# A hybrid attention and recurrence block: queries of six heads as blocks, the first head's gates beside the merge, exponentials ahead of the transposes

## The chip, the cores and the metric

One core of a Trainium2 chip runs the whole layer as one program. The metric is the device time of one execution in microseconds. TensorE (PE) multiplies, ScalarE (ACT) applies functions and copies, VectorE (DVE) does elementwise work and reductions, GpSimd (POOL) does a little of both, and SyncE (SP) issues most of the DMAs. Each engine takes its instructions strictly in the order in which they were written.

## The reference

The layer takes `x` of 1024 tokens by 1024 channels. It computes, in float32:

```
h = rms_norm(x) * norm_w
z = h @ w_in                       # 1024 x 12288: everything below is a slice of z
# branch A: three head groups, 8 heads of 64, (window, dilation) = (128,1), (512,4), (2048,16)
q, k = rms_norm(q)*q_w, rms_norm(k)*k_w
s = q k^T / 8 + bias, banded;  m = max s;  p = exp(s - m);  den = sum p;  o = p v / den
o_a = sum_g(den_g * exp(m_g - max m) * o_g) / sum_g(den_g * exp(m_g - max m))      # the merge
y_a = (o_a * silu(g_a)) @ w_proj_a
# branch B: 8 heads of 128, forward and backward scan, summed
f = lb + (1 - lb) * sigmoid(z_f)
S_t = diag(f_t) S_{t-1} + (1 - f_t) v_t^T ;  o_t = S_t^T q_t                       # in chunks
y_b = (rms_norm(o_fwd + o_bwd) * silu(g_b)) @ w_proj_b
out = x + (sigmoid(zg_a) * y_a + sigmoid(zg_b) * y_b) @ w_out
```

## The kernel before, in words

**Number format.** Every float32 operand of a large product is split into a high part (`hi`, the value rounded to the matmul's float32r) and the rest (`lo`). A product then takes three matmuls, hi by hi, hi by lo, lo by hi. A weight page is 128 by 512 (256 KB). ScalarE makes its `whi`; its `wlo` is made by VectorE, by GpSimd, or by an accumulating DMA, as `b.low` says ("dve", "pool", "dma").

**Direct projections and blocks.** `T_group` and `tok_group` project a group of 128 by 512 outputs in 8 steps of three matmuls (tile `gp`). Other columns of `w_in` go as blocks of 256 columns by all 1024 tokens, in seven quarter-size products instead of eight (`run_quads`, tiles `qA`, `qE`, `qC`), each of 4 x 3 matmuls, with sums of the input prepared once and differences of the weights made in place. The list `blocks` says which: attention's queries and keys (which are then normalised, tile `nss`), merge gates `sg`, recurrence queries `qb` of heads 0 to 3 (`QB = 4`), silu gates `gb` and `ga`. The queries of heads 4 to 7 are projected directly (`evac_qe`).

**Order of work.** One Python program writes the instructions of all engines in one pass. A planner (`Plan`) keeps an estimated time for each engine; `note` holds the costs of instructions. Work beside the main stream is a task with tiles it depends on. `tick` writes a task once its tiles are due within 1.4 us of TensorE's estimated time, and `burst` writes small products between the projection's steps, in order of their kind: transposes (kind 1), values (2), scores (3). In attention (`eager`) there is one burst after each step of three projection matmuls. So costs and due times in the planner decide the order of instructions on an engine, and the hardware then keeps to it.

**Stages.** After the input's preparation and the blocks comes attention, beside the direct projections of the recurrence's inputs (`evac_early`) and of the last heads' queries. A unit of attention is two tiles of 128 queries by four heads: `scores` (matmuls `sc` with 64 rows, bias and row maximum by VectorE), `exps` (ScalarE, four for each half), `transpose_p` (`pT`, copied out to `apt`), `pv` (matmuls `o` with 64 columns). A unit's `exps` waits for `left["turned"] == m`, which holds once all earlier units are transposed. Score tiles come from a ring of four (`s`), two for a unit; values from a ring of 14 (`VR`). Loads for later parts wait for `b.wire()`, the planner's estimate that DMAs are at most 1 us behind.

The merge (`merge_maybe`, `alphas`, `spread_al`) weighs the three groups' outputs: eight steps of three matmuls `al`, three VectorE products, a GpSimd addition, two VectorE operations and a store. Beside it run what is left of the direct projections. Then there is a barrier: `b.until(lambda: mer.get("out", 0) == 8)`, the merge's memory is given back, the recurrence's pools are opened, its lower bounds are computed (a Sigmoid and an Ln, each with its own table on ScalarE), and heads 0 to 7 follow. For each head four groups of forget gates are projected (evacuated into `sk` by `evac_f`); then `start_head` starts the recurrence of that head, which runs beside the next head's gates. The tail multiplies by `w_proj_a`, `w_proj_b`, `w_out`.

TensorE writes to eight PSUM banks, of which the projections have three (`gps`), in attention two; a group's bank is free once ScalarE has copied it out (`stage` or `sk`).

The recorded line of nearly every instruction is 58, that of the helper which passes it on and tells the planner; so the profile is read by tile names.

Of the kernel before, what the change touches and what calls it, by code (L numbers as in the profile page):

```python
# [13 lines left out]
OP = mybir.AluOpType  # L14
# [14 lines left out]
EARLY = 8  # L29
QB = 4  # L30
QRAW, SPARE = 6, 7
LOWS = ("T2", "T4")
SQ, EA = 2, 6
VR, PT = 14, 8

# [80 lines left out]
class Plan:  # L116
# [5 lines left out]
    def __init__(self, nc):  # L122
        self.nc = nc
        self.t = dict(pe=0.0, act=0.0, dve=0.0, pool=0.0, sp=0.0)
        self.port = 0.0
        self.wire = 0.0
        self.w, self.r = Book(), Book()
        self.table = "exp"
        self.wide = True
        self.pe = Engine(self, nc.tensor, "pe")  # L130
        self.act = Engine(self, nc.scalar, "act")
        self.dve = Engine(self, nc.vector, "dve")
        self.pool = Engine(self, nc.gpsimd, "pool")
        self.sp = Engine(self, nc.sync, "sp")
# [7 lines left out]
    def note(self, key, op, args, kw):  # L142
# [30 lines left out]
        else:  # L173
            if key == "pe":
                late = 0.17
                wide = ins[-1].dtype == F32R
                if op == "transpose":
                    pace = 0.109
                elif wide:
                    pace = n / 2400.0 + 0.0133 + (0.0 if self.wide else 0.15)  # L180
                else:
                    pace = 2 * (n / 1200.0 + 0.004)
                    if ins[0].shape[0] <= 64 or ins[0].shape[-1] <= 64:
                        pace /= 2
                self.wide = wide
            elif key == "act":
# [36 lines left out]
class Builder:  # L223
# [35 lines left out]

    def wire(self):  # L260

        return self.p.wire <= self.p.t["pe"] + 1.0

# [321 lines left out]
def hybrid_block(ctx, tc, a, out):  # L585
# [47 lines left out]
    for k in range(6):  # L633
        blocks += qk[2 * k:2 * k + 2] + sg[k:k + 1] + ([("qb", k)] if k % 2 == 0 and k < QB else [])
    blocks += [("gb", k) for k in range(4)] + [("ga", 0), ("ga", 2)]
# [517 lines left out]
    def attention_start(now=False):  # L1153
# [9 lines left out]
        for n, k, shape in (("v", VR, [128, 256]), ("q", 2, [128, 2, S]), ("k", 2, [128, 2, S]),  # L1163
                            ("s", 4, [128, 4, 256]), ("pt", PT, [128, 2, 2, 128]), ("os", 2, [128, 2, 2, 128]),
                            ("bias", 2, [128, 4, 256])):
            att[n] = b.ring(ap, "a" + n, k, shape)
# [4 lines left out]
        for o, g in enumerate((1, 2, 0)):  # L1171
            for hv in range(2):
                soon = lambda n, k=2 * o + hv: att[n].soon() and (k == 0 or b.wire())
                for n, f in (("k", load_k), ("q", load_q), ("bias", load_bias)):
                    b.task("sp", [], lambda g=g, hv=hv, f=f: f(g, hv), 2, lambda n=n, soon=soon: soon(n))
                for i in ((7, 0, 1, 2, 3, 4, 5, 6) if g == 0 else range(8)):
                    b.task("sp", [], lambda g=g, hv=hv, i=i: load_v(g, hv, i), 2, lambda soon=soon: soon("v"))
# [71 lines left out]
    def scores(g, hv, i0):  # L1249
# [22 lines left out]
        for u in range(2):  # L1272
# [8 lines left out]
            v_.tensor_scalar(neg[:, u], mst[g][:, 0, i0 + u, 4 * hv:4 * hv + 4], -1.0, None, op0=OP.mult)  # L1281
            b.task("act", [neg[:, u]], lambda u=u: exps(g, hv, i0, u, ss, neg, geo), 3, lambda: left["turned"] == m)
        left[g, hv] -= 1
# [93 lines left out]

    mctx = ExitStack()
    mer = {}

    def merge_maybe(now=False):
        if mer or not (now or len(stored) == 48) or not att:
            return
        if now:
            b.drain()
        b.eager, b.SLACK = False, 0.6
        psum(3)
        actx.close()
        mer["p"] = mctx.enter_context(tc.tile_pool(name="merge", bufs=1))
        mer["sel"] = sel = mer["p"].tile([128, 3, 4, 128], F32R, name="sel")  # L1390
# [82 lines left out]
    def spread_al(p, half, ld):  # L1473
# [8 lines left out]
        v_.tensor_tensor(nat(ld[1], 2), nat(al[2], 2), per(ld[2], 2), op=OP.mult)  # L1482
        g_.tensor_tensor(ld[0], ld[0], ld[1], op=OP.add)
        v_.tensor_tensor(acc, acc, ld[0], op=OP.add)
# [50 lines left out]
    for h in range(QB, EARLY):  # L1535
# [3 lines left out]
        pos += 2  # L1539
    merge_maybe(True)  # L1540
    for j in range(TAIL, LATE):
        for half in range(2):
            b.run_unit([T_group(pos, half, evac_sg(1, j, half), half == 1)])
        pos += 2
    b.until(lambda: mer.get("out", 0) == 8)
    b.drain()
    mctx.close()

    bctx = ExitStack()
    hp = bctx.enter_context(tc.tile_pool(name="hgrn", bufs=1))
    lbt = hp.tile([128, 2, 2, 8], F32, name="lbt")
    a_.dma_start(lbt, a["lb"])
    mx = hp.tile([128, 2, 8], F32, name="lbm")
    v_.tensor_tensor(mx, lbt[:, 0], lbt[:, 1], op=OP.max)
    for l in range(2):
        v_.tensor_tensor(lbt[:, l], lbt[:, l], mx, op=OP.subtract)
    v_.tensor_tensor(mx, lbt[:, 0], lbt[:, 1], op=OP.subtract)  # L1560
    lb = hp.tile([128, 2, 8], F32, name="lbv")
    omlb = hp.tile([128, 2, 8], F32, name="omlb")
    lomlb = hp.tile([128, 2, 8], F32, name="lomlb")
    a_.activation(lb, mx, AF.Sigmoid)
    v_.tensor_scalar(omlb, lb, -1.0, 1.0, op0=OP.mult, op1=OP.add)
    v_.tensor_scalar(lomlb, omlb, 1e-37, None, op0=OP.max)
    a_.activation(lomlb, lomlb, AF.Ln)
    onw = hp.tile([128, 1], F32, name="onw")
    v_.tensor_scalar(onw, hwc, 1.0 / 256, None, op0=OP.mult)
    mX = hp.tile([128, 128], F32, name="mX")  # L1570
    mY = hp.tile([128, 64], F32, name="mY")
    a_.dma_start(mX, a["c_mx"])
    a_.dma_start(mY, a["c_my"])
    BF = mybir.dt.bfloat16
    rst = hp.tile([128, 512], BF, name="rst")
    g_.memset(rst, 1.0)
    g_.memset(rst.rearrange("p (c t) -> p c t", c=4)[:, :, 0:1], 0.0)
    YB = hp.tile([128, 4, 64], F32, name="YB")
    g_.memset(YB, 0.0)

    ig_ring = b.ring(hp, "ig", 8, [128, 256])
    gb_ring = b.ring(hp, "gb", 3, [128, 512])
    sk_ring = b.ring(hp, "sk", 7, [128, 512])
    qq_ring = b.ring(hp, "q", 2, [128, 512])
# [23 lines left out]
    def load_gb(h, u):  # L1608
        t = gb_ring.get()
        s_.dma_start(t, gbD[h, u])  # L1610
        GB[h, u] = t

    SK, QQ = {}, {}

    def evac_f(h, d, u):
        def f(ps):
            t = sk_ring.get()
            a_.activation(t, ps, AF.Copy)
            b.gps.done(ps)
            SK[h, d, u] = t  # L1620
            if d == 1 and u == 1:
                start_head(h)
        return f

# [281 lines left out]
    for h in range(8):  # L1906
        if h % 2 == 0:
            load_pair(h // 2)
        for u in range(2):
            if h < EARLY:  # L1910
                b.task("sp", [qD], lambda h=h, u=u: load_q_early(h, u), 4, qq_ring.soon)
            b.task("sp", [gbD], lambda h=h, u=u: load_gb(h, u), 4, gb_ring.soon)
        for d in range(2):
            for u in range(2):
                b.run_unit([T_group(pos, u, evac_f(h, d, u), u == 1)])
            pos += 2
        if h >= EARLY:
            for u in range(2):
                b.run_unit([T_group(pos, u, evac_q(h, u), u == 1)])
            pos += 2  # L1920
# [441 lines left out]
```

## Time and profile before

| | |
|---|---|
| time, median of 3 runs | 1475.26 us (1474.36 to 1476.48) |
| the profiled execution's own time | 1474.54 us |
| its span, first to last instruction | 1472.7 us |
| granted TensorE clock, mean | 0.999 |
| busy: TensorE, VectorE, ScalarE, GpSimd | 1454.8, 964.9, 886.8, 382.4 us |
| HBM read and written | 167.98 and 81.43 MB |

Times in the profile count from the first instruction. A row of a group gives its operation, `out<-in` by tile names, shapes, count, busy time, mean duration in ns, and the idle time of the engine just before it with what ended that. Matmuls overlap in the pipeline, so that a row's mean is longer than the distance from one start to the next. A float32 matmul that is not split (`sc`, `o`, `oB`) leaves two records.

### The profile page before, as it was taken

How to read it: one execution, taken by the hardware profiler on the slowest of the kernel's cores; microseconds unless marked ns; L12 is line 12 of the kernel's file. 1: busy time of each engine (PE TensorE's matmuls, PEld its weight loads, DVE VectorE, ACT ScalarE, POOL GpSimd, SP SyncE). 2: the span in 40 equal slices, each digit the busy share in tenths (PEclk: the TensorE clock that was granted, in tenths of full speed). 3: DMA queues.
4: the chain of work that ended last, by engine and by line, in shares of the span. 5: the costliest groups of instructions: out<-in, count | busy, mean ns of one | idle time of the engine just before them, and what ended most of it. 6: DMA issues, size and time to landing. Idle time of an engine off the chain costs nothing. (4 is left out here: it accounts for less than half of the span.)

```text
span 1472.7 us, 22977 instructions
## 1 busy us (share of the span) xinstructions
PE 1454.8 (99%) x7946; PEld 1200.0 (81%) x7946; DVE 964.9 (66%) x1872; ACT 886.8 (60%) x1884; POOL 382.4 (26%) x385
## 2 busy tenths in 40 slices
PE   8999999999999999999999999999999999999998
PEld 7788888877888888887877778888888888788887
DVE  6792576778688876332535536468887976358973
ACT  5543665666576775443778743397777874548461
POOL 0031335454534333332020005332221221001011
PEclk9999999999999999999999999999999999999999
DMA  6465557667632424327657439654444453768565
GB/s 206 134 193 168 171 196 170 155 137 173 151 115 86 122 65 144 115 93 241 210 180 210 132 87 309 203 124 100 130 115 115 104 145 90 225 225 222 183 154 135
DMA packets 193896, 229.44 MB, mean 156 GB/s; under 512 B 45627, under 2 KB 117587, under 8 KB 193268
## 3 DMA queue, kind: packets, MB, share of 16 engines
q1 hardware_dynamic: 179812, 203.93, 43.8%
q0 software_dynamic: 13104, 23.86, 10.6%
q8 instruction: 63, 1.03, 0.3%
q14 instruction: 53, 0.43, 0.1%
q10 hardware_dynamic: 864, 0.19, 0.1%
HBM read 167.98 MB, written 81.43 MB: 169 GB/s over the span
## 5 line engine op out<-in xcount | busy, mean ns | idle before, releaser
L58 POOL TENSOR_TENSOR wlo<-qraw,whi 128x512 fp32r<-128x512 f32 x130 | 190.0, 1467 | 326.2 <-ACT whi L58 288.3
L58 ACT ACTIVATE whi<-qraw 128x512 fp32r<-128x512 f32 x182 | 113.0, 626 | 88.8 <-DVE qraw L58 44.8
L58 DVE TENSOR_TENSOR qraw<-qraw,qraw 128x512 f32<-128x512 f32 x104 | 93.2, 896 | 41.2 <-POOL wlo L58 31.4
L58 PE MATMUL gp<-hh,whi 128*128 128x512 f32 x288 | 118.4, 411 | 0.0
L58 PE MATMUL gp<-hh,wlo 128*128 128x512 f32 x288 | 113.1, 393 | 0.0
L58 PE MATMUL gp<-hl,whi 128*128 128x512 f32 x288 | 112.5, 391 | 0.0
L58 PE MATMUL gp<-whi,hh 128*128 128x512 f32 x248 | 103.0, 415 | 3.0 <-ACT stage L58 1.6
L58 PE MATMUL gp<-whi,hl 128*128 128x512 f32 x248 | 97.7, 394 | 1.3 <-DVE hl L58 1.3
L58 PE MATMUL gp<-wlo,hh 128*128 128x512 f32 x248 | 97.5, 393 | 0.0
L58 ACT ACTIVATE whi<-raw 128x512 fp32r<-128x512 f32 x96 | 59.9, 626 | 47.4 <-PE gp L58 26.7
L58 ACT ACTIVATE as<-as,neg 128x192 f32<-128x192 f32 (+2 forms) x192 | 83.5, 439 | 7.1 <-DVE neg L58 7.1
L58 ACT ACTIVATE stage<-gp 128x512 f32<-128x512 f32 x52 | 30.7, 595 | 87.2 <-PE gp L58 57.5
L58 POOL TENSOR_TENSOR wlo<-raw,whi 128x512 fp32r<-128x512 f32 x40 | 56.0, 1412 | 98.3 <-ACT whi L58 98.2
L58 PE MATMUL qA<-hh,whi 128*128 128x512 f32 x208 | 81.3, 391 | 0.0
L58 PE MATMUL qA<-hh,wlo 128*128 128x512 f32 x208 | 81.3, 391 | 0.0
L58 PE MATMUL qA<-hl,whi 128*128 128x512 f32 x208 | 81.0, 390 | 0.0
L58 DVE SCALAR_TENSOR_TENSOR ny<-ny,spare 128x512 f32<-128x512 f32 x48 | 75.4, 1571 | 1.6
L58 DVE TENSOR_TENSOR wlo<-qraw,whi 128x512 fp32r<-128x512 f32 x52 | 35.9, 690 | 55.3 <-ACT whi L58 55.3
L58 DVE COPY apt<-pT 128x512 f32<-128x512 f32 (+2 forms) x42 | 27.7, 664 | 65.1 <-PE pT L58 65.1
L58 DVE CUSTOM_DVE_ANT_0 as<-sc,abias 128x192 f32<-128x192 f32 (+2 forms) x192 | 56.3, 348 | 20.8 <-PE sc L58 12.3
L58 ACT ACTIVATE ny<-ny 128x512 f32<-128x512 f32 x96 | 60.8, 633 | 12.3 <-DMA qkD<-ny 5.4
L58 PEld LDWEIGHTS gp<-hh,wlo 128*128 128x128 f32 x288 | 54.1, 188 | 11.8
(297 smaller groups left out, 4181.4 us busy)
## 6 DMA issues: line engine op xcount, KB each, us to landing
qraw<-in_w_in_dram SPq DMA_DIRECT2D x104, 256.0 KB, 4.2
raw<-in_w_in_dram SPq DMA_DIRECT2D x88, 256.0 KB, 3.3
qkD<-ny SPq DMA_DIRECT2D x48, 256.0 KB, 2.8
sg<-sgD SPq DMA_DIRECT2D x32, 256.0 KB, 2.9
eraw<-wsD SPq DMA_DIRECT2D x32, 256.0 KB, 3.0
wlo<-in_w_in_dram POOLq DMA_DIRECT2D x31, 256.0 KB, 4.8
sgD<-stage SPq DMA_DIRECT2D x26, 256.0 KB, 2.8
ak<-qkD SPq DMA_DIRECT2D x6, 1024.0 KB, 7.3
```

The lines of the kernel that those rows point to most:

```text
L58: got = f(*args, **kw)
```

## The change

Queries of six heads go as blocks (`QB = 6`), one pair each after the second, third and fourth group of attention blocks; heads 6 and 7 stay direct. The recurrence's first pool, with the bounds, masks and the `sk` ring, is opened beside the merge, which moves to the other side of the memory; the bounds become a task; and head 0's four gate groups are projected before the barrier. After the barrier the other pools are opened and head 0's recurrence starts at once. Attention's `exps` no longer wait for earlier transposes, the score ring has five tiles, the value ring ten, and loads wait only until DMAs are 3.5 us behind. In the merge the addition and the weights' low halves go to VectorE. The planner's cost of a wide matmul after another kind falls from 0.15 to 0.04 us, and changes between half-array and full matmuls cost 0.19 or 0.09 us in it.

```diff
-QB = 4
+QB = 6
-VR, PT = 14, 8
+VR, PT = 10, 8
...
                 wide = ins[-1].dtype == F32R
+                tiled = not wide and op != "transpose" and (ins[0].shape[0] <= 64 or ins[0].shape[-1] <= 64)
...
-                    pace = n / 2400.0 + 0.0133 + (0.0 if self.wide else 0.15)
+                    pace = n / 2400.0 + 0.0133 + (0.0 if self.wide else 0.04)
                 else:
                     pace = 2 * (n / 1200.0 + 0.004)
-                    if ins[0].shape[0] <= 64 or ins[0].shape[-1] <= 64:
+                    if tiled:
                         pace /= 2
-                self.wide = wide
+                if tiled != self.tiled:
+                    pace += 0.19 if wide or self.wide else 0.09
+                self.wide, self.tiled = wide, tiled
...
-    def wire(self):
-        return self.p.wire <= self.p.t["pe"] + 1.0
+    def wire(self, most=1.0):
+        return self.p.wire <= self.p.t["pe"] + most
...
-        blocks += qk[2 * k:2 * k + 2] + sg[k:k + 1] + ([("qb", k)] if k % 2 == 0 and k < QB else [])
+        blocks += qk[2 * k:2 * k + 2] + sg[k:k + 1] + ([("qb", 2 * k - 2)] if 0 < k <= QB // 2 else [])
...
-                            ("s", 4, [128, 4, 256]), ("pt", PT, [128, 2, 2, 128]), ("os", 2, [128, 2, 2, 128]),
+                            ("s", 5, [128, 4, 256]), ("pt", PT, [128, 2, 2, 128]), ("os", 2, [128, 2, 2, 128]),
...
-                soon = lambda n, k=2 * o + hv: att[n].soon() and (k == 0 or b.wire())
+                soon = lambda n, k=2 * o + hv: att[n].soon() and (k == 0 or b.wire(3.5))
...
-            b.task("act", [neg[:, u]], lambda u=u: exps(g, hv, i0, u, ss, neg, geo), 3, lambda: left["turned"] == m)
+            b.task("act", [neg[:, u]], lambda u=u: exps(g, hv, i0, u, ss, neg, geo), 3)
...
         b.eager, b.SLACK = False, 0.6
+        b.low = "dve"
...
-        mer["p"] = mctx.enter_context(tc.tile_pool(name="merge", bufs=1))
+        mer["p"] = mctx.enter_context(tc.tile_pool(name="merge", bufs=1, side="right"))
...
-        g_.tensor_tensor(ld[0], ld[0], ld[1], op=OP.add)
+        v_.tensor_tensor(ld[0], ld[0], ld[1], op=OP.add)
...
     merge_maybe(True)
+    hp = bctx.enter_context(tc.tile_pool(name="hgrn", bufs=1))
...
+    def bounds():
+        v_.tensor_tensor(mx, lbt[:, 0], lbt[:, 1], op=OP.max)
+        for l in range(2):
+            v_.tensor_tensor(lbt[:, l], lbt[:, l], mx, op=OP.subtract)
+        v_.tensor_tensor(mx, lbt[:, 0], lbt[:, 1], op=OP.subtract)
+        a_.activation(lb, mx, AF.Sigmoid)
+        v_.tensor_scalar(omlb, lb, -1.0, 1.0, op0=OP.mult, op1=OP.add)
+        v_.tensor_scalar(lomlb, omlb, 1e-37, None, op0=OP.max)
+        a_.activation(lomlb, lomlb, AF.Ln)
+    b.task("dve", [lbt], bounds, 4, lambda: "ab" in mer)
+    sk_ring = b.ring(hp, "sk", 7, [128, 512])
...
+            if d == 1 and u == 1 and h:
+                start_head(h)
...
+    for d in range(2):
+        for u in range(2):
+            b.run_unit([T_group(pos, u, evac_f(0, d, u), u == 1)])
+        pos += 2
     b.until(lambda: mer.get("out", 0) == 8)
     b.drain()
     mctx.close()
...
+    hp = bctx.enter_context(tc.tile_pool(name="hgrn2", bufs=1))
...
+        if h == 0:
+            start_head(0)
+            continue
         for d in range(2):
             for u in range(2):
                 b.run_unit([T_group(pos, u, evac_f(h, d, u), u == 1)])
```

More of the change, by code (lines that the diff above doesn't have):

```diff
@@ L128, in __init__ @@
         self.table = "exp"
-        self.wide = True
+        self.wide, self.tiled = True, False
         self.pe = Engine(self, nc.tensor, "pe")
@@ L1375, in vuse @@
         return sum(1 for i in range(8) for _, _, v, _ in geometry(g, i)[3] if v == vt)
-    mctx = ExitStack()
+    mctx, bctx = ExitStack(), ExitStack()
     mer = {}
@@ L1540, in hybrid_block @@
     merge_maybe(True)
+    hp = bctx.enter_context(tc.tile_pool(name="hgrn", bufs=1))
+    lbt = hp.tile([128, 2, 2, 8], F32, name="lbt")
+    lb, omlb, lomlb = (hp.tile([128, 2, 8], F32, name=n) for n in ("lbv", "omlb", "lomlb"))
+    onw = hp.tile([128, 1], F32, name="onw")
+    mX = hp.tile([128, 128], F32, name="mX")
+    mY = hp.tile([128, 64], F32, name="mY")
+    rst = hp.tile([128, 512], BF, name="rst")
+    YB = hp.tile([128, 4, 64], F32, name="YB")
+    mx = hp.tile([128, 2, 8], F32, name="lbm")
+    a_.dma_start(lbt, a["lb"])
+    a_.dma_start(mX, a["c_mx"])
+    a_.dma_start(mY, a["c_my"])
+    g_.memset(rst, 1.0)
+    g_.memset(rst.rearrange("p (c t) -> p c t", c=4)[:, :, 0:1], 0.0)
+    g_.memset(YB, 0.0)
+    v_.tensor_scalar(onw, hwc, 1.0 / 256, None, op0=OP.mult)
+    def bounds():
[9 more added lines that the diff above has]
+    sk_ring = b.ring(hp, "sk", 7, [128, 512])
     for j in range(TAIL, LATE):
@@ L1544, in hybrid_block, with evac_f, f @@
         pos += 2
+    SK, QQ = {}, {}
+    def evac_f(h, d, u):
+        def f(ps):
+            t = sk_ring.get()
+            a_.activation(t, ps, AF.Copy)
+            b.gps.done(ps)
+            SK[h, d, u] = t
+            if d == 1 and u == 1 and h:
+                start_head(h)
+        return f
+    for d in range(2):
+        for u in range(2):
+            b.run_unit([T_group(pos, u, evac_f(0, d, u), u == 1)])
+        pos += 2
     b.until(lambda: mer.get("out", 0) == 8)
@@ L1547, in hybrid_block @@
     mctx.close()
[L1552 to L1579, printed above, removed]
+    hp = bctx.enter_context(tc.tile_pool(name="hgrn2", bufs=1))
     ig_ring = b.ring(hp, "ig", 8, [128, 256])
     gb_ring = b.ring(hp, "gb", 3, [128, 512])
-    sk_ring = b.ring(hp, "sk", 7, [128, 512])
     qq_ring = b.ring(hp, "q", 2, [128, 512])
@@ L1611, in load_gb @@
         GB[h, u] = t
[L1613 to L1623, printed above, removed]
     def evac_q(h, u):
```

## The prediction

> **What bounds the kernel now.** I read the page's totals first, then TensorE's waits, the busy time by stage, the timeline around the largest waits, and last the groups of the attention and merge stages. The totals:
>
> ```profile
> span 1472.7 us, 22977 instructions
> ...
> PE 1454.8 (99%) x7946; PEld 1200.0 (81%) x7946; DVE 964.9 (66%) x1872; ACT 886.8 (60%) x1884; POOL 382.4 (26%) x385
> ```
>
> TensorE is idle for 17.9 us of 1472.7. A busy TensorE need not be at its peak, so the pace inside comes next. In the block stage these two matmuls stand five products of twelve, that is 60 matmuls, apart (start, then duration):
>
> ```profile
> 640.54 0.39 PE L58 MATMUL qA<-S1h,whi 128*128 128x512 f32 x1
> ...
> 654.14 0.39 PE L58 MATMUL qA<-hh,whi 128*128 128x512 f32 x1
> ```
>
> 13.60 / 60 = 0.227 us each: the 0.39 of a row is latency, 0.227 is what a 512-column matmul costs. By stage (stretch, its length, busy time of PE, PEld, DVE, ACT, POOL; clock; DMA share; GB/s):
>
> ```profile
> 152.00:673.00 521.00, 517.37 (x2267) 424.79 (x2266) 352.95 (x419) 317.95 (x544) 216.00 (x164) 1.00 0.50 135
> 673.00:691.40 18.40, 16.96 (x74) 13.41 (x72) 1.37 (x2) 4.86 (x7) 2.35 (x5) 1.00 0.74 254
> 691.40:868.40 177.00, 175.99 (x1585) 141.00 (x1585) 91.77 (x476) 130.67 (x470) 13.80 (x20) 1.00 0.55 175
> 868.40:934.60 66.20, 65.51 (x292) 53.84 (x292) 39.86 (x47) 17.60 (x33) 29.05 (x22) 1.00 0.83 252
> 934.60:980.00 45.40, 45.16 (x200) 37.01 (x199) 21.34 (x39) 30.06 (x54) 15.32 (x22) 1.00 0.62 160
> 980.00:1268.00 288.00, 286.68 (x2033) 248.55 (x2031) 224.30 (x494) 211.18 (x460) 63.59 (x104) 1.00 0.47 119
> ```
>
> These are blocks, hand-over to attention, attention, merge, the first head's gates, the rest of the recurrence. TensorE fills each, so a change is worth the TensorE time it takes away, plus idle it closes, minus idle it opens. The named idle is small:
>
> ```profile
> PE gp L58 <- ACT stage L58: 2.2, 3, 0.8
> PE nss L58 <- ACT whi L58: 1.6, 1, 1.6
> PE nss L58 <- DVE nlo L58: 1.2, 2, 0.9
> ```
>
> **Six heads' queries in blocks.** Today heads 4 and 5 are projected directly: 2 heads x 2 halves x 8 steps x 3 = 96 matmuls of 512. As a third query block they take 7 products x 4 x 3 = 84. Saving: 12 x 0.227 = **2.7 us**. The four page loads and four stores of 256 KB stay; the block splits 7 pages instead of 4 and adds 4 differences on VectorE and its evacuations. These lie under 84 x 0.227 = 19.1 us of matmuls, in a stage where DVE is busy 352.95 and ACT 317.95 of 521; if that cover were gone, TensorE would wait as it does there now, 521.00 - 517.37 = 3.6 us over 26 blocks, or 0.1 us for one more. Moving the query blocks behind other blocks reshuffles those 3.6 us: it can save them or add as much again. I take 0, nearest the 0.1.
>
> **Exponentials ahead, five score tiles, loads let go earlier.** The ACT queue now holds a unit's exponentials until all earlier units are transposed. Attention has 3 groups x 2 halves x 4 = 24 units, 177.0 / 24 = 7.4 us each; ACT's busy time would allow 130.67 / 24 = 5.4. But TensorE does not idle there: it fills with projections, three matmuls after each burst of attention work (241 in this stage, so 80 bursts, 3.3 per unit):
>
> ```profile
> 691.40:868.40 177.00, 71.23 (x241) 40.61 (x241) 0.00 (x0) 6.40 (x11) 1.00 0.55 175
> ```
>
> That row is the stretch again, for the projections' own instructions. A piece of its timeline:
>
> ```profile
> 719.71 0.40 PE L58 MATMUL gp<-whi,hl 128*128 128x512 f32 x1
> 720.04 1.97 PE L58 MATMUL o<-apt,av 128*64 128x128 f32 x32
> 721.93 0.50 PE L58 MATMUL gp<-whi,hh 128*128 128x512 f32 x1
> 722.27 0.39 PE L58 MATMUL gp<-wlo,hh 128*128 128x512 f32 x1
> ```
>
> So shortening attention moves projections from inside it to behind it and by itself saves nothing. What it can save is the price of going in and out: the matmul before `o` takes 0.33 instead of 0.227, the first one after it 0.34, together 0.21 us per excursion into the half-array matmuls (scores and `o`). [...] There are at most 24 score runs and 24 `o` runs, and in these rows each stands alone between projections, so the count cannot grow and a loss by this term is excluded. If units went at ACT's 5.4 us, bursts would fall by 80 x (1 - 5.4/7.4) = 22; I take half, 10 excursions, because a score run and an `o` run must be ready in the same burst to share one: 10 x 0.21 = **2.1 us**, bounds 0 and 24 x 0.21 = 5.0. Fewer value tiles (10 for 14) cost nothing: ten are still eight ahead of the two that a unit reads, four units or 30 us. The planner's new costs for mode changes issue nothing; they only move work, inside these bounds.
>
> **First head's gates beside the merge.** The 96 gate matmuls move ahead of the barrier, 96 query matmuls have left from there, so the merge keeps its eight groups of cover behind the input projections. What leaves the barrier is this chain:
>
> ```profile
> 946.84 1.28 ACT L58 ACT_TABLE_LOAD   x1 [9.55 <-issue]
> 949.49 0.22 ACT L58 ACTIVATE lbv<-lbm 128x16 f32<-128x16 f32 x1 [1.37 <-DVE lbm L58]
> 949.72 1.28 ACT L58 ACT_TABLE_LOAD   x1
> 951.99 0.60 ACT L58 ACTIVATE sk<-gp 128x512 f32<-128x512 f32 x1 [0.76 <-DMA ig<-ibD]
> ```
>
> ```profile
> 952.01 0.39 PE L58 MATMUL gp<-hh,wlo 128*128 128x512 f32 x1
> 952.64 0.50 PE L58 MATMUL gp<-hbh,whi 128*128 128x512 f32 x1 [0.24 <-ACT sk L58]
> ```
>
> (ACT, then TensorE.) ACT stands still for 9.55 us until the merge's memory is free, then loads two tables, and the gates' first evacuation waits behind all that until 951.99; with three banks TensorE runs out of room and loses 952.64 - 952.01 - 0.227 = **0.4 us**. Now the bounds' DMAs (three on ACT's queue), seven VectorE operations, two table loads and GpSimd's memsets are issued beside the merge, where ACT is busy 17.60 of 66.2; behind them on ACT wait evacuations that have three banks, 3 x 24 x 0.227 = 16 us. I take 0.4 saved; 0 if the first Ln of the gates waits for the same memory, as long. Head 0's loads on SP's queue (eight of 128 KB, four of 256 KB, 2.1 MB) used to be issued ahead of its gates; now its recurrence starts at the barrier with them. At the 160 GB/s of 934.60:980.00 they take 13 us; the next head's gates, 96 x 0.227 = 21.8 us, cover that, and what would be late is head 0's products, not a projection.
>
> **No GpSimd in the merge.** Fifteen low halves and eight adds go to VectorE:
>
> ```profile
> L58 DVE TENSOR_TENSOR wlo<-qraw,whi 128x512 fp32r<-128x512 f32 x52 | 35.9, 690 | 55.3 <-ACT whi L58 55.3
> ```
>
> ```profile
> L58 POOL TENSOR_TENSOR wlo<-raw,whi 128x512 fp32r<-128x512 f32 x15 | 21.0, 1413 | 12.0 <-ACT whi L58 12.0
> ...
> L58 POOL TENSOR_TENSOR og<-og,og 128x512 f32<-128x512 f32 x7 | 9.0, 1287 | 21.8 <-DVE og L58 21.8
> ```
>
> ```profile
> L58 DVE TENSOR_TENSOR macc<-macc,og x7: 691/1764/1766, 892.7 to 935.1; 128x512 f32<-128x512 f32 x7
> ```
>
> (The first from the page, two groups of the merge stage, and the accumulating tile, min/median/max ns.) At 0.69 us each that is 23 x 0.69 = 16 us on top of 39.86 of 66.2: it fits, and the accumulate, 0.69 alone but 1.76 at the median beside GpSimd, should fall. Cost 0, covered by the eight groups; without cover, VectorE's lag (rival C).
>
> **Sum:** -2.7 + 0 - 2.1 - 0.4 + 0 = -5.2 us. The profiled execution took 1474.54 (span 1472.7 and 1.84 around it), so 1469.3; the median lies 0.72 above it, so **1470.1**.
>
> **Rivals.** *A: only the matmuls count.* Attention keeps its excursions and the barrier's 0.4 us returns with the recurrence's own memory: 1475.26 - 2.7 = 1472.5. For it: nothing in attention is idle to be filled, and bursts with both runs ready need five free banks of six. Against it: the chain at the barrier does leave.
>
> *B: slower, ACT gets in TensorE's way.* In attention the projections have two banks, and a pair of groups takes both:
>
> ```profile
> 767.83 0.58 ACT L58 ACTIVATE aos<-o 128x512 f32<-128x512 f32 x1
> 768.31 1.06 ACT L58 ACTIVATE stage<-gp 128x512 f32<-128x512 f32 x2
> 768.94 0.50 PE L58 MATMUL gp<-whi,hh 128*128 128x512 f32 x1 [0.82 <-ACT stage L58]
> ```
>
> ```profile
> L58 ACT ACTIVATE as<-as,neg 128x192 f32<-128x192 f32 x80 | 35.2, 444 | 7.1 <-DVE neg L58 7.1
> ...
> L58 ACT ACTIVATE stage<-gp 128x512 f32<-128x512 f32 x11 | 6.4, 591 | 6.2 <-PE gp L58 5.4 <-DMA ibD<-stage 0.7
> ```
>
> Exponentials issued early stand in front of these evacuations: 4 x 0.44 = 1.8 us for each half unit. Behind a pair TensorE waits at once; behind a single group it waits once the evacuation is later than the next group's own 24 x 0.227 = 5.4 us, so from three half units in front of it. If half the 1.8 falls on each of the 11 evacuations: 11 x 0.9 = 9.9, so 1472.5 + 9.9 = 1482.4. Against it: ACT is free for a quarter of the stage.
>
> *C: slower, the merge is no longer hidden.* Its VectorE chain already ends 10 us behind TensorE's last `al`:
>
> ```profile
> 933.84 0.85 PE L58 MATMUL al<-alB,sel 128*128 128x512 f32 x3
> ```
>
> ```profile
> 944.25 0.32 SPq L58 DMA_DIRECT2D oaD<-macc  x1
> ```
>
> With ACT's hold of 12 us (934.6 to 946.84) grown by 10 us, the three banks' 16 us are passed by 6: 1472.5 + 6 = 1478.5. Against it: VectorE has 10 us to spare and sheds the contention.
>
> **Chances:** forecast 0.61, A 0.26, B 0.08, C 0.05. Under 0.2% (3 us) this kernel's measurements cannot be told from no change; A falls inside that, at 0.18%. Faster 0.59, same 0.28, slower 0.13. Low end: 1475.3 less 2.7, 5.0 and most of the 3.6 of block idle gives 1465; high end: A with 3.6 us more idle, 1476.
>
> **What would show it.** Block products: `qA<-hh,whi` 216 instead of 208, the direct projections 96 fewer. Attention shorter than 177 us with fewer than 241 projections inside; if `o` and score runs still each stand between projections, the 2.1 us are wrong. The first `sk` evacuation within a microsecond of its group, beside the merge. No GpSimd adds, `macc<-macc,og` near 0.69. I am wrong if idle of TensorE grows past 17.9 us, or if evacuations (`stage`, `sk`) show up as its longest waits.

## The result, and the profile after

| | before | after |
|---|---|---|
| time, median of 6 runs | 1475.56 us (1474.36 to 1476.48) | 1466.14 us (1465.86 to 1468.61) |
| ratio, 95% interval | | 0.9939 (0.9926 to 0.9952) |
| the profiled execution's own time | 1474.54 us | 1465.98 us |
| its span | 1472.7 us | 1464.2 us |

The change saves 9.4 us in the medians (1475.56 - 1466.14) and 8.5 us between the two profiled spans; 1470.1 was forecast. The page's totals after:

```profile
span 1464.2 us, 22916 instructions
...
PE 1448.2 (99%) x7934; PEld 1197.8 (82%) x7934; DVE 983.5 (67%) x1905; ACT 883.2 (60%) x1883; POOL 348.4 (24%) x362
```

TensorE has 12 records fewer, as counted, and is still the bound: idle for 16.0 us (17.9 before). By stage, in the columns used before: blocks, hand-over, attention, merge, what stands between it and the first recurrence product, and the recurrence with the tail's first products:

```profile
152.00:691.40 539.40, 536.02 (x2351) 440.63 (x2350) 364.94 (x428) 324.03 (x555) 218.23 (x169) 1.00 0.50 135
691.40:708.80 17.40, 16.66 (x73) 13.25 (x71) 1.35 (x2) 4.86 (x7) 2.60 (x6) 1.00 0.70 243
708.80:869.00 160.20, 160.07 (x1534) 132.26 (x1533) 92.54 (x476) 126.38 (x467) 13.56 (x19) 1.00 0.58 190
869.00:926.30 57.30, 56.61 (x256) 46.54 (x253) 44.51 (x67) 15.25 (x29) 1.76 (x4) 1.00 0.90 269
926.30:968.40 42.10, 42.10 (x187) 34.81 (x186) 22.42 (x41) 27.30 (x50) 5.75 (x10) 1.00 0.50 141
968.40:1304.80 336.40, 334.30 (x2231) 285.22 (x2230) 245.36 (x527) 232.25 (x495) 64.18 (x105) 1.00 0.50 131
```

The stretches are of different length because work has moved. They can be compared once each wide matmul in them is taken off at 0.227 us. For that, the projections alone, in attention and in the recurrence after, and both rows of the recurrence before (all instructions, then projections):

```profile
708.80:869.00 160.20, 55.63 (x190) 32.03 (x189) 0.00 (x0) 4.60 (x8) 1.00 0.58 190
...
968.40:1304.80 336.40, 246.41 (x967) 174.47 (x966) 10.13 (x15) 19.52 (x33) 1.00 0.50 131
```

```profile
979.90:1313.30 333.40, 331.58 (x2226) 284.83 (x2224) 245.27 (x525) 233.43 (x495) 63.59 (x104) 1.00 0.50 131
```

```profile
979.90:1313.30 333.40, 241.57 (x962) 174.56 (x960) 10.34 (x15) 19.63 (x33) 1.00 0.50 131
```

| where the 8.5 us are | worked out from the rows | us |
|---|---|---|
| 84 block matmuls for 96 direct ones | 12 x 0.227 | -2.7 |
| blocks, apart from the new block | 539.40 - 521.00 - 84 x 0.227 | -0.7 |
| hand-over to attention | 17.40 - 18.40 | -1.0 |
| attention, apart from projections | (160.20 - 190 x 0.227) - (177.00 - 241 x 0.227) = 117.1 - 122.3 | -5.2 |
| merge and first gates, beyond their matmuls | after: 99.4 for 435 wide and 8 transposes (99.6); before: 111.6 for 484 and 8 (110.7) | -1.1 |
| recurrence, apart from projections | (336.40 - 967 x 0.227) - (333.40 - 962 x 0.227) = 116.9 - 115.0 | +1.9 |

The sum is -8.8, within the 0.3 us that border records and missing records leave open. Two rows need care. Of the 1.1 us in the merge and the gates only 0.2 is idle time that went (before, 66.20 - 65.51 and 45.40 - 45.16; after, 57.30 - 56.61 and 0); the rest is the restart behind the wait at the barrier (before, 0.40 us are lost there with 0.24 of it idle, and the first matmul behind it takes 0.34 instead of 0.227, from 952.64 to 952.98), and the counting of records that lie across a border, at 0.227 us each. And of the 5.2 us in attention 0.9 is idle time that went (177.00 - 175.99 before, 160.20 - 160.07 after). More than half of the whole is in attention, and the recurrence got worse. What changed in attention is seen in a piece of its timeline:

```profile
736.48 1.91 PE L58 MATMUL pT<-ident,as 128*128 128x128 f32 x16
738.32 1.97 PE L58 MATMUL o<-apt,av 128*64 128x128 f32 x32
740.22 1.57 PE L58 MATMUL sc<-ak,aq 64*128 64x192 f32 x16
741.72 0.50 PE L58 MATMUL gp<-whi,hh 128*128 128x512 f32 x1
742.06 0.40 PE L58 MATMUL gp<-wlo,hh 128*128 128x512 f32 x1
```

A unit's transposes come as 16, then outputs and the next scores in one piece, then three projections. Before, score runs and output runs stood apart from each other, between projections or transposes: 47 runs of half-array matmuls in attention. Now there are 30 (counted in the traces).

TensorE's longest waits after the start:

```profile
PE qA L58 <- ACT spare L58: 2.6, 1, 2.6
...
PE gp L58 <- ACT stage L58: 1.4, 2, 0.7
...
PE oB L58 <- DVE S L58: 0.7, 1, 0.7
PE qA L58 <- ACT stage L58: 0.5, 2, 0.3
PE nss L58 <- DVE nlo L58: 0.3, 1, 0.3
```

The waits for `nss` have shrunk from 3.6 us to 0.3, the one for the first scores (0.7) is gone, and a new one of 2.6 us stands in the blocks. In the merge, without GpSimd, the two VectorE steps that had taken up to 1.77 us are all alike:

```profile
L58 DVE TENSOR_TENSOR macc<-macc,og x8: 691/692/693, 886.7 to 931.5; 128x512 f32<-128x512 f32 x8
L58 DVE TENSOR_TENSOR macc<-macc,gal x8: 691/692/693, 887.5 to 932.2; 128x512 f32<-128x512 f32 x8
```

Before the change, `macc<-macc,og` took 1.76 or 1.77 us in six of eight cases. In each of them a GpSimd `wlo` of 1.29 us had begun 0.07 or 0.08 us earlier; in the two that took 0.69 GpSimd stood still. One of each, from the timeline before:

```profile
921.15 1.29 POOL L58 TENSOR_TENSOR wlo<-raw,whi 128x512 fp32r<-128x512 f32 x1
921.22 1.77 DVE L58 TENSOR_TENSOR macc<-macc,og 128x512 f32<-128x512 f32 x1 [1.39 <-POOL og L58]
...
926.55 1.28 POOL L58 TENSOR_TENSOR og<-og,og 128x512 f32<-128x512 f32 x1 [0.92 <-DVE og L58]
927.87 0.69 DVE L58 TENSOR_TENSOR macc<-macc,og 128x512 f32<-128x512 f32 x1 [1.40 <-POOL og L58]
```

So a step beside a GpSimd operation took 1.07 us longer here, most of that operation's length.

### The profile page after: what moved, and what is told of

Its sections match the earlier page's. It is cut to its first block, busy times and chain, and to the rows that moved or that the text cites. A ratio compares the mean times of both kernels' runs of the same rounds, so it can differ in the third digit from the quotient of the medians.

```text
span 1464.2 us, 22916 instructions
## 1 busy us (share of the span) xinstructions
PE 1448.2 (99%) x7934; PEld 1197.8 (82%) x7934; DVE 983.5 (67%) x1905; ACT 883.2 (60%) x1883; POOL 348.4 (24%) x362
## 4 chain that ended last, share of the span: by engine, by line
PE 86%; DVE 6%; ACT 3%; DMA 3%; issue 1%; SPq 1%; DVEq 0%; ACTq 0%
PE gp L58 29%; PE qA L58 18%; PE qE L58 9%; PE sA L58 6%; PE sE L58 5%; PE qC L58 4%; PE o L58 3%; PE oB L58 3%; PE pT L58 2%; PE sc L58 2%; PE nss L58 1%; PE U L58 1%; DMA qraw<-in_w_in_dram 1%; DVE Bc L58 1%; DVE S L58 1%
## 5 line engine op out<-in xcount | busy, mean ns | idle before, releaser
L58 POOL TENSOR_TENSOR wlo<-qraw,whi 128x512 fp32r<-128x512 f32 x135 | 194.2, 1443 | 342.2 <-ACT whi L58 307.1
L58 ACT ACTIVATE whi<-qraw 128x512 fp32r<-128x512 f32 x189 | 117.4, 626 | 101.4 <-DVE qraw L58 48.8
L58 DVE TENSOR_TENSOR qraw<-qraw,qraw 128x512 f32<-128x512 f32 x108 | 98.3, 911 | 44.8 <-POOL wlo L58 26.9
L58 PE MATMUL gp<-hh,whi 128*128 128x512 f32 x264 | 109.7, 416 | 0.0
L58 PE MATMUL gp<-hh,wlo 128*128 128x512 f32 x264 | 103.7, 393 | 0.0
L58 PE MATMUL gp<-hl,whi 128*128 128x512 f32 x264 | 103.0, 390 | 0.0
L58 POOL COPY mm<-Bc 128x8 f32<-128x8 f32 x64 | 32.5, 538 | 206.0 <-DVE Bc L58 123.9
L58 DVE SCALAR_TENSOR_TENSOR ny<-ny,spare 128x512 f32<-128x512 f32 x48 | 67.0, 1397 | 1.6
L58 PEld LDWEIGHTS gp<-whi,hh 128*128 128x128 f32 x248 | 46.8, 189 | 19.1 <-issue 5.0
L58 DVE TENSOR_TENSOR nlo<-ny,nhi 128x512 fp32r<-128x512 f32 x48 | 52.8, 1103 | 9.6 <-ACT nhi L58 9.6
```

Source lines behind the costliest of these rows:

```text
L58: got = f(*args, **kw)
```

## The experiments

Each was timed beside the kernel before on its own chip, whose median was 1474.9, 1475.6 and 1474.9 us in the three sets (1475.6 beside the changed kernel), so that a difference between kernels of two sets is uncertain by some 0.7 us.

### What an excursion costs: scores kept apart from outputs

```diff
-                      lambda: left["in"] < 3 and att["s"].soon(2), banks=4 if g < 2 else 2)
+                      lambda: not b.p.tiled and left["in"] < 3 and att["s"].soon(2), banks=4 if g < 2 else 2)
```

> The changed kernel with one more condition on a unit's scores: they are not written directly behind half-array matmuls, so a score run and an output run never share an excursion. All work and all other edits stay; the instruction order has 47 runs of half-array matmuls in attention instead of 30 (before the change: 47). Theory (excursions): attention's 4.9 us came from 17 fewer excursions at 0.29 us; 17 come back, so 1466.1 + 4.9 = 1471. Rival (exponentials themselves, or a shorter attention, freed TensorE): stays at 1466 to 1467.

Measured: 1473.12 us, ratio 0.9984 (0.9975 to 0.9993), 7.0 more than the changed kernel. Attention, all instructions and then projections alone:

```profile
709.10:886.80 177.70, 177.30 (x1592) 142.14 (x1591) 92.18 (x476) 129.09 (x470) 13.52 (x19) 1.00 0.54 175
```

```profile
709.10:886.80 177.70, 73.02 (x248) 41.67 (x247) 0.00 (x0) 6.52 (x11) 1.00 0.54 175
```

177.70 - 248 x 0.227 = 121.4, against 117.1: 4.3 us for 17 runs, 0.25 each. The rest of the 7 us is outside attention: the wait in the blocks was 0.6 us longer in this execution, and a wait of 2.0 us came before the first `kT`. So the theory holds for attention, in place and nearly in size; the whole kernel moved by more. The same account for ten kernels (runs counted in the trace, length and projections from the same two views):

| kernel | runs | length, us | projections | rest at 0.227 each |
|---|---|---|---|---|
| before | 47 | 177.0 | 241 | 122.3 |
| apart | 47 | 177.7 | 248 | 121.4 |
| no_ahead | 41 | 178.4 | 260 | 119.4 |
| rings | 34 | 172.6 | 242 | 117.7 |
| ahead_alone | 33 | 178.4 | 264 | 118.5 |
| ahead_and_merge | 33 | 178.2 | 264 | 118.3 |
| old_costs | 32 | 170.1 | 227 | 118.6 |
| after | 30 | 160.2 | 190 | 117.1 |
| gates_late | 30 | 160.3 | 191 | 116.9 |
| four_heads | 30 | 161.4 | 189 | 118.5 |

The other four lie with their like: 116.6 to 116.9 for 30 runs, 119.9 for the 41 of `no_ahead_gates_late`. The rest follows the runs and not the length (178 us with 118.5, 170 with 118.6). What is off the line is mostly idle time, the length less TensorE's busy time: 1.2 us in `four_heads`, 1.0 before, 0.9 in `old_costs`, 0.4 in `apart`, at most 0.2 in the others of the table. Without it the 17 runs are worth 4.3 us between `before` and `after` and 4.1 between `apart` and `after`, 0.24 to 0.25 each.

Two parts of that price are seen at every run in the traces of `before`, `apart` and `after`. The wide matmul ahead of a run takes 0.33 us (where a transpose stands there, it takes 0.20 instead of 0.11), and the first wide one behind it 0.34: together 0.21, so 17 runs are 3.6 us. The end of a run is not among what joining saves: 32 records of `o` take 1.90 us up to the scores behind them after the change (738.32 to 740.22), and 1.89 up to a projection before it (720.04 to 721.93). The other 0.5 to 0.7 us is not accounted for.

### The exponentials alone, and with the merge's edit

```diff
-            b.task("act", [neg[:, u]], lambda u=u: exps(g, hv, i0, u, ss, neg, geo), 3, lambda: left["turned"] == m)
+            b.task("act", [neg[:, u]], lambda u=u: exps(g, hv, i0, u, ss, neg, geo), 3)
```

This one edit in the kernel before:

> The kernel before with one edit alone: exponentials do not wait for earlier transposes. Its order has 33 runs instead of 47. Theory (excursions): 14 x 0.29 = 4.1 us less, 1471.5. Rival (the gain needs the fifth score tile, the planner's costs or the early loads as well): 1475. Rival (ACT gets in the way of evacuations): above 1475.6.

Measured: 1479.67 us, ratio 1.0034 (1.0021 to 1.0047): slower. In attention the theory held (122.3 to 118.5, 0.8 of it idle time), but the gain was lost behind it, at the end of the merge:

```profile
929.91 1.68 PE L58 MATMUL al<-alB,sel 128*128 128x512 f32 x5
936.48 0.79 PE L58 MATMUL al<-alB,sel 128*128 128x512 f32 x1 [4.88 <-DVE og L58]
937.07 0.63 PE L58 MATMUL gp<-hh,whi 128*128 128x512 f32 x1
937.50 0.63 PE L58 MATMUL gp<-hl,whi 128*128 128x512 f32 x1
```

TensorE waits 4.88 us for VectorE's merge steps, and the matmuls after it follow at 0.43 us instead of 0.227, at a granted clock of 0.50: eight of them, 1.6 us, until the clock is back. The table suggests why: attention took about as long as before but held 264 projections instead of 241, so that fewer were left to cover the merge. This run alone does not show that; the two runs with the longer attention below, which differ only in that cover, do show what it is worth. None of the three expectations had this, though the total is one that the third allowed.

The same with the merge's two edits for VectorE (addition and low halves):

> The kernel before with two edits: exponentials do not wait for earlier transposes, and the merge does without GpSimd. Theory (what made the exponentials alone slower is the merge's chain, 7 us of wait and half-pace matmuls): these go, the 14 excursions' 3.9 us stay: 1475 - 3.9 = 1471. Rival (an earlier exponential costs elsewhere, or the merge's end is late for its loads rather than for VectorE): 1475 to 1480.

Measured: 1474.73 us, ratio 1.0000 (0.9991 to 1.0010). The merge without GpSimd took back 4.9 us of the loss, and the wait for `al` fell from 4.9 to 1.7 us. 1471 was not reached: in the profiled execution (1473.3) there are that 1.7 us, and 1.7 us before the first scores where the kernel before has 0.7.

### The wait for transposes put back in the changed kernel

```diff
+            b.task("act", [neg[:, u]], lambda u=u: exps(g, hv, i0, u, ss, neg, geo), 3, lambda: left["turned"] == m)
-            b.task("act", [neg[:, u]], lambda u=u: exps(g, hv, i0, u, ss, neg, geo), 3)
```

> The changed kernel with one edit undone: a unit's exponentials wait again for all earlier transposes. Its order has 41 runs of half-array matmuls in attention instead of 30, and 258 projection matmuls inside attention instead of 189. Theory (excursions at 0.27 us, and the gates now cover the merge, since only 150 query and input matmuls are left for it): 11 x 0.27 = 3.0 us more, 1469.1. Rival (the shorter attention matters by itself): more than 1471.

Measured: 1471.65 us, ratio 0.9973 (0.9964 to 0.9983), 5.5 more. Attention's share is 119.4 - 117.1 = 2.3. In this execution (1473.37) the block wait was 3.5 us with eight matmuls at half pace behind it, and 2.0 us went before the first `kT`; those are outside attention, and the runs spread from 1469.3 to 1473.8. The size expected for attention (3.0) is about right, the total is not: it is the one the rival named, and the 2.0 us before `kT`, which come with a longer attention as the next experiment says, are in its favour.

### Score and value rings as before

```diff
-VR, PT = 10, 8
+VR, PT = 14, 8
-                            ("s", 5, [128, 4, 256]), ("pt", PT, [128, 2, 2, 128]), ("os", 2, [128, 2, 2, 128]),
+                            ("s", 4, [128, 4, 256]), ("pt", PT, [128, 2, 2, 128]), ("os", 2, [128, 2, 2, 128]),
```

> The changed kernel with four score tiles and fourteen value tiles as before. Its order has 34 runs and 240 projection matmuls in attention. Theory (the fifth tile shortens attention and lets a score run stand behind an output run): 4 x 0.27 = 1.1 us more, the longer attention alone nothing, 1467.2. Rival (a shorter attention is worth something by itself): 1469 or more.

Measured: 1470.64 us, ratio 0.9975 (0.9962 to 0.9987), 4.5 more; expected 1.1. Attention's rest is 0.6 more, where four runs were priced at 1.1; again the block wait (3.1 us, eight slow matmuls) and 2.0 us before the first `kT`, likewise followed by slow ones, make the total, which is again the rival's. That last wait is found in the three kernels (`apart`, `no_ahead`, `rings`) whose longer attention pushes the merge farthest into the gates (last `al` at 947 to 951 us), and in none of the others (943 in `old_costs`, 926 in the changed kernel). In `rings` VectorE ends the merge's steps at 956 us and comes to the `sk` steps that `kT` waits for at 969.29; in `old_costs` the two are at 949 and 966.89. So the trace speaks for the rival: here a shorter attention is worth something by itself, through the merge that then ends earlier.

### The gates behind the barrier, with a short and with a long attention

```diff
-    for d in range(2):
-        for u in range(2):
-            b.run_unit([T_group(pos, u, evac_f(0, d, u), u == 1)])
-        pos += 2
     b.until(lambda: mer.get("out", 0) == 8)
...
-        if h == 0:
-            start_head(0)
-            continue
```

> The changed kernel with the first head's four gate groups back behind the barrier; pools, bounds and all else stay as changed. Theory (the merge needs these 22 us as cover): between the end of attention and the barrier 35 us of projections are left for a merge that took 57 us; its steps can be written closer, 5 us of VectorE each, so some 12 + 40 us; TensorE waits 10 to 17 us: 1476 to 1483. Rival (attention's earlier end is cover enough): 1466 to 1468.

Measured: 1465.65 us, ratio 0.9940 (0.9926 to 0.9954). The theory fell, and the rival fits within 0.4 us: the gates do not have to stand before the barrier. The rows of the changed kernel say why. Ahead of its gates stand 20 groups, 480 matmuls; the hand-over takes 72, attention 190, and the stretch up to the last `al` the remaining 218 (its 256 records are those, 24 `al`, 8 transposes and a few at the borders). So the last merge step is written with the last query group, and the gates stand behind it, beside the merge's last VectorE steps at most.

With the wait for transposes as well, attention holds 260 projections and 150 are left:

> The same, and the first head's four gate groups back behind the barrier, so that 150 matmuls (34 us) lie between the end of attention and the merge's last step, where the changed kernel has 219. Theory (the gates are cover that only a longer attention needs): the merge took 48 to 57 us, so TensorE waits 10 to 20 us, in part at half pace: 1479 to 1489, where without the wait for transposes the late gates cost nothing. Rival (the merge can be as short as its cover): 1469 to 1471.

Measured: 1483.01 us, ratio 1.0052 (1.0037 to 1.0067), 11.4 more than with the gates before the barrier. TensorE's longest waits, and the stretch of the merge (0.90 is the granted clock):

```profile
PE al L58 <- DVE og L58: 8.7, 5, 3.2
...
PE al L58 <- DVE macc L58: 1.3, 2, 0.8
```

```profile
888.30:942.70 54.40, 43.81 (x182) 33.76 (x183) 42.43 (x70) 16.78 (x31) 1.76 (x4) 0.90 0.95 281
```

The merge needs some 50 us behind attention (an estimate from its stretch, 57.30 us in the changed kernel and 54.40 here), and here finds 150 x 0.227 = 34. The gates are cover that a longer attention needs and this one doesn't.

### GpSimd back in the merge

```diff
-        b.low = "dve"
-        v_.tensor_tensor(ld[0], ld[0], ld[1], op=OP.add)
+        g_.tensor_tensor(ld[0], ld[0], ld[1], op=OP.add)
```

> The changed kernel with GpSimd back in the merge: it makes the addition of each step and the low halves of the weights that are split there. Attention's order is the same (30 runs). Theory (the merge's VectorE chain is what the eight groups have to cover, and GpSimd slows it): with the exponentials-alone kernel TensorE waited 4.9 us for that chain and then ran 8 matmuls at half pace; here it waits 2 to 6 us at the merge's end, 1468 to 1472. Rival (the merge is hidden either way, the edit is free): 1466.1, within 0.7.

Measured: 1468.66 us, ratio 0.9958 (0.9943 to 0.9974); the runs go from 1465.7 to 1469.9. The total lies in the theory's range, but not for its reason: TensorE waits in the merge, for the chain that was named, only 0.9 us of the 2 to 6 expected:

```profile
PE qA L58 <- ACT spare L58: 2.8, 1, 2.8
...
PE al L58 <- DVE og L58: 0.9, 1, 0.9
```

The rest is the block wait, with 14 matmuls at half pace behind it in the profiled execution (1469.85). The intervals of this kernel and the changed one overlap, so the total is unclear; the wait of 0.9 us is what the edit is seen to remove here.

### Four heads as blocks

```diff
-QB = 6
+QB = 4
```

> The changed kernel with queries of four heads as blocks instead of six; the runs of half-array matmuls stay at 30. Theory (matmul count): 12 matmuls of 0.227 come back, 1466.1 + 2.7 = 1468.9. Rival (the block stage gained or lost more by the blocks' new order): differs from that by over 1 us, up to 2.6 us lower if the new wait at 301 us goes with the third query block.

Measured: 1471.52 us, ratio 0.9978 (0.9969 to 0.9987), 5.4 more where 2.7 were expected. The rival's sign was wrong: the wait did not go but grew to 3.4 us, and slow matmuls follow it, though the instructions up to there are those of the changed kernel:

```profile
300.22 0.39 PE L58 MATMUL qC<-hh,wlo 128*128 128x512 f32 x1
304.01 0.50 PE L58 MATMUL qA<-S2h,whi 128*128 128x512 f32 x1 [3.40 <-ACT spare L58]
...
305.50 0.63 PE L58 MATMUL qA<-S2h,wlo 128*128 128x512 f32 x1
305.93 0.63 PE L58 MATMUL qA<-S2h,whi 128*128 128x512 f32 x1
```

The first scores also wait 1.5 us for their values (`av`); every kernel with four heads has such a wait, 0.7 to 1.7 us, and none with six. Why the place of the last query block decides that was not tried. So 2.7 us is the matmuls' price by count, and the waits with the slow matmuls are 3.6 us more in the profiled execution (1472.28 - 1465.98 - 2.7).

### The planner's costs

```diff
-                    pace = n / 2400.0 + 0.0133 + (0.0 if self.wide else 0.04)
+                    pace = n / 2400.0 + 0.0133 + (0.0 if self.wide else 0.15)
-                if tiled != self.tiled:
-                    pace += 0.19 if wide or self.wide else 0.09
```

> The changed kernel with the planner's old costs for matmuls of another kind (0.15 for a wide one behind another, nothing for half-array changes). Attention's runs are 32 instead of 30. Theory (the costs only move work; the recurrence's 1.7 us of extra time is due to them): 2 x 0.29 = +0.6 in attention, -1.7 in the recurrence, 1465.0. Rival (the costs are what made the rest fit): above 1467.5.

Measured: 1466.80 us, ratio 0.9945 (0.9933 to 0.9957): not told from the changed kernel. The two shares are there, of opposite sign. Recurrence, all instructions and projections:

```profile
969.20:1304.20 335.00, 333.30 (x2232) 285.71 (x2230) 245.92 (x528) 232.97 (x495) 63.85 (x105) 1.00 0.50 131
```

```profile
969.20:1304.20 335.00, 243.28 (x968) 175.59 (x966) 10.34 (x15) 19.65 (x33) 1.00 0.50 131
```

335.00 - 968 x 0.227 = 115.3 instead of 116.9: 1.6 us less. Attention's rest is 118.6 instead of 117.1: 1.5 more, half of it idle time (170.10 - 169.24), where two runs more had been priced at 0.6. So the new costs gain in attention what they lose in the recurrence. What they do there can be counted in the traces: other products break into the projections 92 times in the changed kernel's stretch, 80 times here and 79 in the kernel before.

### The wait at 301 us

In the changed kernel, SP's queue, then VectorE and ScalarE at the page in question:

```profile
286.49 0.64 SPq L58 DMA_DIRECT2D skewD<-tabD  x1
287.22 10.42 SPq L58 DMA_DIRECT2D qraw<-in_w_in_dram  x4
```

```profile
301.32 0.69 DVE L58 TENSOR_TENSOR qraw<-qraw,qraw 128x512 f32<-128x512 f32 x1 [9.84 <-DMA qraw<-in_w_in_dram]
302.05 0.63 ACT L58 ACTIVATE whi<-qraw 128x512 fp32r<-128x512 f32 x1 [7.94 <-DVE qraw L58]
302.58 0.58 ACT L58 ACTIVATE spare<-qE 128x512 f32<-128x512 f32 x1
```

Four weight pages are issued right behind a copy of the third group's bias table from DRAM to DRAM, and VectorE stands still for 9.84 us until one has landed. ScalarE waits for VectorE with that page's `whi`, and the copies to `spare`, for which TensorE waits at 301 us, stand behind it.

```diff
-                    after=b.p.t["pe"] + 3.0 + 100.0 * g + 10.0 * k)
+                    after=b.p.t["pe"] + 3.0 + (0.0, 100.0, 400.0)[g] + 10.0 * k)
```

> The changed kernel with the third group's two bias-table copies (DRAM to DRAM, 768 KB each) issued 300 us later, where the DMA engines are a third busy. Theory (the page that TensorE waits for at 301 us, 2.75 us, and 3.4 to 3.6 us with slow matmuls behind it in two of the experiments, is late because of these copies and the query stores): the wait goes, 1466.1 - 2.75 = 1463.4 or lower. Rival (the page is late because of the weight sums' accumulating DMAs): within 0.7 of 1466.1.

Measured: 1463.64 us, ratio 0.9927 (0.9914 to 0.9940); its runs (1462.55 to 1464.44) all lie below the changed kernel's. The wait is gone: the longest for `qA` is now this.

```profile
PE qA L58 <- ACT stage L58: 0.2, 1, 0.2
```

So the wait needs the copies, and of the theory's 2.75 us 2.5 are confirmed. The edit moves them by some 200 us (from 277 and 286 us to 479), not the 300 of the expectation; that is far enough for what it tests (the DMA share of the changed kernel is 0.26 from 470 to 490 us). In the kernel before, the same copies stood at 272 and 286 us and TensorE waited for no page, so that they are not enough by themselves. The stores of the query block, which the move of that block brought to the same time, may share in it; they were not moved apart from it.

### All three together

```diff
+        self.new = True
-                    pace = n / 2400.0 + 0.0133 + (0.0 if self.wide else 0.04)
+                    pace = n / 2400.0 + 0.0133 + (0.0 if self.wide else 0.04 if self.new else 0.15)
-                if tiled != self.tiled:
+                if self.new and tiled != self.tiled:
...
         b.eager, b.SLACK = False, 0.6
+        b.p.new = False
```

with the later copies and the gates behind the barrier.

> The changed kernel with the third group's bias-table copies 300 us later, the planner's old costs from the merge on, and the first head's gates behind the barrier. Theory: 1463.6 (copies later), less 1.4 for the recurrence's order (its time above the wide matmuls was 116.0 instead of 117.4 with the old costs), less at most 0.5 for the gates: 1462. Rival (the recurrence's gain came from something else): 1463.6.

Measured: 1463.27 us, ratio 0.9918 (0.9903 to 0.9933), the lowest of all, but not the 1462 expected; its difference from the copies alone is inside the intervals. The recurrence's length says that the order did improve, 333.40 - 961 x 0.227 = 115.3:

```profile
967.00:1300.40 333.40, 331.60 (x2225) 284.63 (x2224) 245.12 (x525) 232.87 (x495) 63.57 (x104) 1.00 0.50 131
```

```profile
967.00:1300.40 333.40, 241.54 (x961) 174.36 (x960) 10.33 (x15) 19.63 (x33) 1.00 0.50 131
```

In the same execution what stands behind that stretch took 0.9 us longer than with the copies alone (1460.7 - 1300.4 = 160.3 against 1461.3 - 1301.9 = 159.4), half of it a wait of 0.44 us before the tail's first `sE`, so that 0.6 us of span remain (1460.7 against 1461.3).

## Why the prediction was right, and where it was not

- **The total.** The forecast was 4.0 us too high. Attention gave 3.1 more than its term, the blocks' order and the hand-over 1.7 that had no term or one of 0, and the recurrence took 1.9 back. So the time is inside the range with two terms about right and three that partly cancel.
- **What bounds the kernel.** Right: TensorE stays at 99%, and what could be accounted for in these kernels is its matmuls, their pace, changes between half-array and full matmuls, and waits.
- **Twelve matmuls, 2.7 us.** Right in number. That moving the query blocks costs 0 was right in sum (-0.7) and wrong in kind: the `nss` waits went (3.6 to 0.3 us) and the page wait of 2.6 us came. It is the longest of all and bears an evacuation's name (`spare`), which looks like the prediction's sign of being wrong, but it goes back to the page. The bound of 3.6 us for reshuffled idle held.
- **The hand-over.** Not counted: 1.0 us went there, 0.7 of it the wait before the first scores, which none of the kernels with six heads in blocks has. Why is open.
- **Attention, 2.1 us.** The mechanism was right, the term was mis-sized: 5.2 us between the profiles, 4.3 where the runs alone were put back. What failed is the count, 17 instead of 10. The price of 0.21 held: the matmul ahead and the first one behind are as slow in the changed kernel as in the quoted rows, which makes 3.6 us for 17 runs. The next part, 0.9 us, is idle time in attention that went; the prediction's own row has 177.00 and 175.99, but rival A says that nothing there is idle to be filled. That the price goes with the count of runs, attention's share in `apart` shows (4.3 us for 17); why a matmul beside a run takes 0.10 or 0.11 us longer, no run shows. That shortening attention saves nothing by itself was too strong: it decides how much cover the merge has, and in `rings`, `no_ahead` and `apart` a longer one went with 2.0 us before `kT`.
- **"Exponentials ahead" as the cause.** Half right. Alone they gave 33 runs and a slower kernel; the fifth score tile, early loads and costs together shortened attention from 178 to 160 us (172.6 with the rings as before, 170.1 with the old costs; the early loads were not tried alone), and that left the merge more cover.
- **Gates beside the merge, 0.4 us.** The 0.4 us was gained, but not by the gates: with the gates back behind the barrier (`gates_late`) it stayed gained. What cleared the barrier is then what else left it, the bounds' chain with the pool it needs; no run put those back. That the gates make up the merge's cover for the 96 query matmuls that left was wrong: they stand behind its last step, and it has what attention leaves, 218 matmuls.
- **No GpSimd, cost 0.** Right that it costs nothing; the gain was not counted: about 0.9 us here, and 4.9 us where the merge is short of cover.
- **Not foreseen:** the recurrence's 1.9 us. "The planner's new costs issue nothing; they only move work, inside these bounds" was the step that failed; moved work is worth some 1.5 us either way, in the recurrence by breaking into the projections 13 times more.
- **Rivals.** A lost: attention's runs did fall. B did not happen: the waits for `stage` went from 2.2 to 1.4 us. C, at 0.05, is the one the experiments produced, in `ahead_alone` (1479.67) and `no_ahead_gates_late` (1483.01), near the 1478.5 worked out for it. That nearness is luck: its condition was a longer hold of ScalarE, and what uncovered the merge was too few projections left behind attention.

## What to carry to other kernels

Where one engine is busy all the time and runs two kinds of work, price the changes between the kinds and count them; what makes both kinds ready together can be worth more than the work removed (here 5.2 us in attention against 2.7 for 12 matmuls). Work that fills a stage is also cover for the next one, so before an edit moves it, count what is left behind and what it has to hide (the gates behind the barrier cost nothing in `gates_late` and 11.4 us with the longer attention). Look at bulk copies that nobody waits for: here they made a page late (14.0 us from issue to landing, where 4.0 is the median), and in some kernels the wait cost more than itself (5.0 us for 3.4 in `four_heads`).

## What the runs showed of the hardware

Behind a wait of TensorE the matmuls can follow at 0.427 us instead of 0.227, where the profile gives a granted clock of 0.50: eight of them behind the 4.88 us of `ahead_alone`, so that a stall of 3.4 us in `four_heads`, also with eight, cost 5.0. At the same place, waits of 2.6 us (the changed kernel), 2.7 (`old_costs`), 2.8 (`gates_late`, `no_ahead_gates_late`) and 3.2 (`apart`) had no slow matmuls behind them, while 2.8 (`gpsimd_merge`, 14 slow), 3.1 (`rings`), 3.4 (`four_heads`) and 3.5 (`no_ahead`) had. Nor is 2.8 us the least: the 2.04 us before the first `kT` had slow matmuls behind them in `rings` and none in `apart` and `no_ahead`, and near the start of the kernel before, waits of 0.88 and 1.45 us that stand 2.5 us apart are followed by six (granted clock 0.50 from 33.12 to 36.50 us). So waits of one length, 2.8 and 2.04 us, went either way in these runs, and no run shows what decides it.
